# Value products in two matmuls instead of three, a yield in the block sums, and the first head's loads in another order

## The chip, the cores and the metric

The kernel runs on one core of one Trainium2 chip. The metric is device time in microseconds. The kernel before took a median of 2062.04 us over three runs (2061.18 to 2064.16).

## The reference

The program computes a two-layer block over 1024 latent tokens of width 1024, with 256 context tokens ahead of them. The first layer is a bidirectional mLSTM, the second a pooling mixer. The change lies in the first layer, in float32:

```python
def headwise(x, w):                       # w: blocks of 4 x 4
    return jnp.einsum("btgi,gio->btgo", xb, w).reshape(bsz, t, e)

xm, z, og = jnp.split(h @ w_in, 3, axis=-1)
xc = jax.nn.silu(short_conv(xm, conv_w, conv_b))
q = headwise(xc, w_q); k = headwise(xc, w_k) * DH ** -0.5
v = headwise(xm, w_v)
pre = concat([q, k, v]) @ w_g + b_g       # gates: log_i and log_sigmoid
# then, per head, a scan over tokens in both directions with q, k, v and the gates
```

So for each of the 16 blocks of 128 inner channels, 1280 tokens are multiplied by a 128 x 128 block-diagonal matrix (the value) and by 16 columns that give the value's part of the gates.

## The kernel before

**Precision.** A float32 product is made of three matmuls on rounded halves: high by high, high by low, low by high (`mm3`, lines 148 to 151, through `mm`, line 137). `load_w` (lines 139 to 146) loads a weight block and splits it: ACT copies the high half (L143), VectorE (DVE) subtracts it (L145).

**Stage.** The change's first two parts lie in the loop over n = 0 to 15, one n for each block of 128 inner channels. `features(n)` multiplies the weight block with all tokens in three pieces, ci = 0 and 1 of 512 columns and ci = 2 of 256, each 8 steps of k with three matmuls, into PSUM tiles "pa" (three buffers). Each piece is copied by ACT to `xp` (L367) and split into `xmh` (ACT L369) and `xml` (DVE L370). Then follows a convolution along tokens: ACT L372, DVE L373 and L374, ACT L375, and another split (L382, L383). Stores to memory go through the SP queue. Three accumulators `gacc` in "pc" take the gates' columns, six matmuls after each n.

**Tokens.** `token_part(n)` is a generator, stepped from inside `features(n + 1)` (every second k; at n = 2, where two tokens' work is waiting, every k). It goes over ten tiles s of 128 tokens. For each, three matmuls with the token tile as the weights and 144 columns moving (128 of the value matrix, 16 of the gates) fill a third of a PSUM tile "pb" (two buffers). After three s the tile is emptied: ACT copies the high half (L409), DVE subtracts for the low half (L410) and adds the gate columns into `pre` (L411). Both halves are stored (L413).

**Sums.** `block_sums` prepares sums of blocks of h for a later stage: for k = 0 to 3 it loads two tiles (L508), combines them on DVE (L510 to L513), and splits and stores four results (L517 to L519). The loop steps it twice for each n from 2 on. Its tiles, and the token tiles `xmh`, `xml`, come from one pool "S4" of 32 buffers; `xp`, the convolution's result and the value's halves come from "T5", which has five.

**Order.** Each engine runs its instructions strictly in the order of its own queue. That order is not the order of the code: the framework puts each instruction in by its own estimate of when its operands are there, and where a buffer is used again its new user waits for the old one's last reader. So the order of an engine's queue is read from the compiled program.

**First head.** After the stage, `start_head(0)` loads the first 512 tokens of head 0 (L677), `make_A` builds a matrix on DVE, `next_q` makes the queries (L720, L721), the gates' rows are loaded (L691, L698), then the rest of the tokens (`finish_x`, L677 and L671), then values (L685). Scores go into "pa", and DVE multiplies them by the decays (L740) that ACT makes from the gates' rows (L754 to L758).

Of the kernel before, what the change touches and what calls it, by code (L numbers as in the profile page):

```python
# [12 lines left out]
F32R = mybir.dt.float32r  # L13
AF = mybir.ActivationFunctionType
ALU = mybir.AluOpType
AX = mybir.AxisListType

P = 128
# [34 lines left out]
def hybrid_block(ctx: ExitStack, tc: tile.TileContext, xT, ctxT, vecs, w_ada0, w_ada, w_blk, w_krow, blk_mask, w_gate, w_in, b_gate, w_out,  # L53
                 bw_in, bw_pool, bw_out, inv_cnt, outT):
    nc = tc.nc
    V, S, G, PE = nc.vector, nc.scalar, nc.gpsimd, nc.tensor
# [7 lines left out]
    def nm(s):  # L64
        uid[0] += 1
        return f"{s}_{uid[0]}"
# [11 lines left out]
    def tl(tag, shape, dt=F32):  # L78
        n = int(np.prod(shape[1:])) * 4
        assert n <= BYTES[tag], (tag, shape)  # L80
        pool = ph["pool"] if tag in PHASED else sb
        return pool.tile(list(shape), dt, tag=tag, bufs=BUFS[tag], name=nm(tag))
# [3 lines left out]
    def pt_(tag, shape=(P, 512)):  # L86
        return ps.tile(list(shape), F32, tag=tag, bufs=PBUFS[tag], name=nm(tag))
# [4 lines left out]
    def f(t):  # L92
        return t.bitcast(F32)

    def const1(shape, name, dt=F32):
        return ph["pool"].tile(list(shape), dt, name=name)

    def small1(shape, tag, bufs=2, dt=F32):
        return ph["pool"].tile(list(shape), dt, tag=tag, bufs=bufs, name=nm(tag))
# [25 lines left out]
    vh_d = dr.tile([NH, P, 10, DH], F32, name="vh_d")  # L125
    vl_d = dr.tile([NH, P, 10, DH], F32, name="vl_d")
# [9 lines left out]
    def mm(out, lhsT, rhs, start, stop):  # L136
        PE.matmul(out, lhsT, rhs, start=start, stop=stop)  # L137
# [10 lines left out]
    def mm3(out, wh, wl, xh, xl, first, last):  # L148
        mm(out, wh, xh, first, False)
        mm(out, wh, xl, False, False)  # L150
        mm(out, wl, xh, False, last)
# [62 lines left out]
    for kind in LOADS:  # L214
        if kind == "x":
            t = tl("S4", [P, T])
            nc.sync.dma_start(t, xT[:, len(x_sb)])
            x_sb.append(t)
        elif kind == "c":
            t = tl("S4", [P, 4, TC])  # L220
# [13 lines left out]
    for k in range(2):  # L234
# [13 lines left out]
    pre = const1([P, 10, 16], "pre")  # L248
    G.tensor_tensor(pre, bg[:, None, :].to_broadcast([P, 10, 16]), zero1[:, :, None].to_broadcast([P, 10, 16]),
                    op=ALU.add)  # L250
# [138 lines left out]
    def token_part(n, xmh, xml, xch, xcl):  # L389

        bv = small1([P, 32, 4], "bv", 1)
        V.tensor_tensor(bv, mask, wb[:, 2, n:n + 1].to_broadcast([P, 32, 4]), op=ALU.mult)
        bv = bv.rearrange("p a b -> p (a b)")
        vv = small1([P, 2, 144], "vv", dt=F32R)
        V.tensor_copy(vv[:, 0, :P], bv)
        V.tensor_tensor(vv[:, 1, :P], bv, f(vv[:, 0, :P]), op=ALU.subtract)
        V.tensor_copy(vv[:, :, P:], f(gm_all[:, n]).rearrange("p (a b) -> p a b", a=2))
        vh, vl = tl("T5", [P, 10, P], F32R), tl("T5", [P, 10, P], F32R)
        for s0, s1 in ((0, 3), (3, 6), (6, 9), (9, 10)):
            p = pt_("pb", [P, 3, 144])  # L400
            for s in range(s0, s1):
                yield
                if s < 8:
                    ah, al = xmh[0][:, s * P:(s + 1) * P], xml[0][:, s * P:(s + 1) * P]
                else:
                    ah, al = xmh[1][:, (s - 8) * P:(s - 7) * P], xml[1][:, (s - 8) * P:(s - 7) * P]
                mm3(p[:, s - s0], ah, al, vv[:, 0], vv[:, 1], True, True)
            q = p[:, :s1 - s0]
            S.activation(vh[:, s0:s1], q[:, :, :P], AF.Copy)  # L409
            V.tensor_tensor(vl[:, s0:s1], q[:, :, :P], f(vh[:, s0:s1]), op=ALU.subtract)  # L410
            V.tensor_tensor(pre[:, s0:s1], pre[:, s0:s1], q[:, :, P:], op=ALU.add)  # L411
        for t, dst in ((vh, vh_d), (vl, vl_d)):
            nc.sync.dma_start(dst[n // 4, :, :, (n % 4) * P:(n % 4 + 1) * P], f(t))  # L413
        yield

        gx = gx_all[:, n]
        for ci, (o, w) in enumerate(CHUNKS):
            ch, cl = (xch[0][:, o:o + w], xcl[0][:, o:o + w]) if ci < 2 else (xch[1], xcl[1])
            if n == 0:
                mm(gacc[ci][:32, :w], gx, ch, True, False)  # L420
                mm(gacc[ci][:16, :w], gx[:, :16], cl, False, False)
            else:
                mm(gacc[ci][:16, :w], gx[:, :16], cl, False, False)
                mm(gacc[ci][:32, :w], gx, ch, False, n == KE - 1)
# [78 lines left out]
    def block_sums():  # L503

        for k in range(4):
            t0, t1 = tl("S4", [P, T]), tl("S4", [P, T])
            for t, kk in ((t0, k), (t1, k + 4)):
                nc.sync.dma_start(t, h_d[kk])  # L508
            b11, b12, b21, b22 = t0[:, :512], t0[:, 512:], t1[:, :512], t1[:, 512:]
            V.tensor_tensor(b22, b22, b12, op=ALU.subtract)  # L510
            V.tensor_tensor(b12, b12, b11, op=ALU.subtract)
            V.tensor_tensor(b11, b22, b11, op=ALU.add)
            V.tensor_tensor(b21, b21, b11, op=ALU.subtract)  # L513
            yield
            for j, x in ((2, b11), (3, b22), (1, b12), (4, b21)):
                t = tl("S4", [P, 2, 512], F32R)
                S.activation(t[:, 0], x, AF.Copy)  # L517
                V.tensor_tensor(t[:, 1], x, f(t[:, 0]), op=ALU.subtract)
                nc.sync.dma_start(t_d[j - 1, k], f(t))  # L519
                yield  # L520

    side, parts, sums = iter(()), [], block_sums()
    with ctx0:
        for n in range(KE):
            out = features(n, side)
            for _ in side:
                pass
            if n == 2:
                bilinear()
            if n >= 2:  # L530
                for _ in range(2):
                    next(sums, None)
            parts.append(token_part(n, *out))
            if n:
                side = chain(*parts)
                parts = []
# [165 lines left out]
    def make_A(h):  # L702
        ah, al = tl("wh", [P, 4, 32, 4], F32R), tl("wl", [P, 4, 32, 4], F32R)
        r = tl("wr", [P, 4, 32, 4])
        for c in range(4):
            V.tensor_tensor(r[:, c], mask, amat[:, 4 * h + c:4 * h + c + 1].to_broadcast([P, 32, 4]), op=ALU.mult)
        V.tensor_copy(ah, r)
        V.tensor_tensor(al, r, f(ah), op=ALU.subtract)
        return ah.rearrange("p c a b -> p c (a b)"), al.rearrange("p c a b -> p c (a b)")
# [113 lines left out]
    def start_head(h):  # L823
        hd = {}
        fetch_x(hd, h, 0)
        return dict(h=h, hd=hd)

    def next_q(cur, tp):
        return make_q(cur["hd"], cur["A"], tp)

    def finish_x(cur):
        for ci in (1, 2):
            fetch_x(cur["hd"], cur["h"], ci)

    cur = start_head(0)
    cur["A"] = make_A(0)
    cur["q"] = next_q(cur, 0)
    cur["rc"], cur["R"] = load_ctx_gates(0), load_gates(0)
    finish_x(cur)
    fetch_v(cur["hd"], 0, 0, 5)  # L840
    st_prev = st_now = nxt = None
    for i in range(len(seq) + 1):
# [42 lines left out]
        if st and ti == 7:  # L885
            cur = nxt
# [299 lines left out]
    for e, i, n0, n1 in ((V, 0, 0, 4), (G, 1, 2, 4), (V, 1, 0, 2)):  # L1186
        t = yo[i][:, n0:n1]
# [84 lines left out]
```

## Time and profile before

| what | value |
|---|---|
| median of three runs | 2062.04 us |
| the profiled execution's own time | 2061.71 us |
| its span, first to last instruction | 2059.9 us |
| mean granted TensorE clock, share of full | 0.986 |
| TensorE (PE) busy | 1993.8 us, 97% |
| VectorE (DVE) busy | 1244.8 us, 60% |
| ScalarE (ACT) busy | 760.5 us, 37% |
| hardware DMA queue, share of 16 engines | 48.8% |
| chain of waits, share by PE | 87% |

The span is one execution by the hardware profiler, and 1.8 us of the profiled run lie around it. In the timelines a row is one instruction or several equal ones in a row (x2, x3), with its start, its duration and, in brackets, how long its engine was idle before it and what ended that. Matmuls overlap, so that the pace of a stream is read from starts, not from durations.

### The profile page before, as it was taken

How to read it: one execution, taken by the hardware profiler on the slowest of the kernel's cores; microseconds unless marked ns; L12 is line 12 of the kernel's file. 1: busy time of each engine (PE TensorE's matmuls, PEld its weight loads, DVE VectorE, ACT ScalarE, POOL GpSimd, SP SyncE). 2: the span in 40 equal slices, each digit the busy share in tenths (PEclk: the TensorE clock that was granted, in tenths of full speed). 3: DMA queues.
4: the chain of work that ended last, by engine and by line, in shares of the span. 5: the costliest groups of instructions: out<-in, count | busy, mean ns of one | idle time of the engine just before them, and what ended most of it. 6: DMA issues, size and time to landing. Idle time of an engine off the chain costs nothing.

```text
span 2059.9 us, 26957 instructions
## 1 busy us (share of the span) xinstructions
PE 1993.8 (97%) x10210; PEld 1680.1 (82%) x10210; DVE 1244.8 (60%) x2115; ACT 760.5 (37%) x1225; POOL 325.9 (16%) x399
## 2 busy tenths in 40 slices
PE   7899999999999899999999999999999999999997
PEld 5678788888888688888888878887888888888897
DVE  4866566677777577667676662444747293844444
ACT  5444454433333432333323322433423131223443
POOL 4400000042232000000000001343000000001265
PEclk9999999999999999999999999999999999999999
DMA  8476776864444854648355334534331312133573
GB/s 322 159 255 222 261 241 214 303 196 138 148 129 133 269 181 141 227 132 273 98 166 207 108 97 144 197 114 163 103 104 50 102 51 92 46 126 130 181 242 124
DMA packets 201986, 339.48 MB, mean 165 GB/s; under 512 B 12508, under 2 KB 116444, under 8 KB 201856
## 3 DMA queue, kind: packets, MB, share of 16 engines
q1 hardware_dynamic: 201856, 337.76, 48.8%
q8 instruction: 80, 1.31, 0.3%
q14 instruction: 50, 0.41, 0.1%
HBM read 234.77 MB, written 102.94 MB: 164 GB/s over the span
## 4 chain that ended last, share of the span: by engine, by line
PE 87%; DVE 3%; DMA 3%; POOL 1%; ACT 1%; issue 1%; SPq 0%; DVEq 0%; ACTq 0%; POOLq 0%
PE pa L137 45%; PE pc L137 33%; PE pb L137 7%; PE pb L781 1%; DMA wr<-in_w_ada_dram 1%; POOL hn L969 1%; PE pc L812 1%; DVE S L901 1%; DVE wl L145 1%; DMA wr<-in_w_in_dram 1%; DMA T<-in_bw_out_dram 0%; DMA S<-xl_d 0%; POOL S L989 0%; DVE wl L658 0%; DMA S<-h_d 0%
## 5 line engine op out<-in xcount | busy, mean ns | idle before, releaser
L137 PE MATMUL pa<-S,wh 128*128 128x512 f32 (+1 forms) x2496 | 725.9, 375 | 13.8 <-DVE S L312 7.1
L137 PEld LDWEIGHTS pa<-S,wh 128*128 128x128 f32 x2496 | 447.4, 191 | 88.6 <-DVE S L312 10.8
L137 PE MATMUL pa<-S,wl 128*128 128x512 f32 (+1 forms) x1248 | 462.5, 371 | 3.3 <-DVE wl L145 3.3
L137 PE MATMUL pc<-S,wh 128*128 128x512 f32 (+1 forms) x1616 | 451.4, 365 | 4.4 <-ACT wh L143 3.5
L137 PEld LDWEIGHTS pc<-S,wh 128*128 128x128 f32 x1616 | 292.7, 189 | 54.3 <-ACT wh L143 3.7
L145 DVE TENSOR_TENSOR wl<-wr,wh 128x1024 fp32r<-128x1024 f32 (+1 forms) x124 | 147.5, 1189 | 273.0 <-ACT wh L143 272.1
L137 PE MATMUL pc<-S,wl 128*128 128x512 f32 (+1 forms) x808 | 293.8, 365 | 1.0 <-DVE wl L145 1.0
L137 PEld LDWEIGHTS pa<-S,wl 128*128 128x128 f32 x1248 | 237.6, 190 | 44.0 <-DVE wl L145 3.7
L137 PE MATMUL pa<-S,S 128*128 128x512 f32 (+1 forms) x1152 | 250.9, 363 | 10.1 <-DMA S<-xh_d 5.8
L143 ACT ACTIVATE wh<-wr 128x1024 fp32r<-128x1024 f32 (+1 forms) x124 | 124.6, 1005 | 368.6 <-PE pa L137 148.3
L137 PE MATMUL pc<-S,pt 128*128 128x512 f32 x960 | 227.4, 391 | 1.5 <-DVE S L721 1.1
L137 PEld LDWEIGHTS pa<-S,S 128*128 128x128 f32 x1152 | 191.8, 190 | 40.2 <-DMA S<-xh_d 6.2
L137 PEld LDWEIGHTS pc<-S,pt 128*128 128x128 f32 x960 | 178.2, 188 | 38.5 <-DVE S L721 1.7
L137 PEld LDWEIGHTS pc<-S,wl 128*128 128x128 f32 x808 | 152.9, 189 | 25.7 <-DVE wl L145 1.8
L783 ACT ACTIVATE pt<-pb 128x512 fp32r<-128x512 f32 (+1 forms) x96 | 47.7, 523 | 213.8 <-PE pb L781 208.0
L969 POOL TENSOR_TENSOR hn<-hn,pt 128x512 f32<-128x512 f32 (+1 forms) x48 | 77.5, 1617 | 309.0 <-ACT pt L968 307.9
L740 DVE SCALAR_TENSOR_TENSOR T<-pa,T 128x256 f32<-128x256 f32 (+3 forms) x184 | 78.2, 454 | 33.5 <-PE pa L137 29.3
L137 PE MATMUL pb<-S,wh 128*128 128x512 f32 x256 | 78.8, 389 | 0.0
L570 ACT ACTIVATE wh<-T 128x512 fp32r<-128x512 f32 x70 | 41.2, 627 | 96.4 <-PE pc L137 78.3
L794 DVE BATCH_NORM_STATS2 st<-pc 128x6 f32<-128x512 f32 x32 | 22.4, 699 | 86.4 <-PE pc L137 86.4
L145 DVE TENSOR_TENSOR wl<-T,wh 128x1024 fp32r<-128x1024 f32 x32 | 45.5, 1421 | 47.3 <-ACT wh L143 47.2
L137 PEld LDWEIGHTS pb<-vv,S 128*128 128x128 f32 x384 | 61.6, 190 | 11.8 <-ACT S L369 1.9
(319 smaller groups left out, 2371.5 us busy)
## 6 DMA issues: line engine op xcount, KB each, us to landing
wr<-in_bw_in_dram SPq DMA_DIRECT2D x40, 512.0 KB, 3.5
wr<-in_w_in_dram SPq DMA_DIRECT2D x34, 512.0 KB, 4.9
wr<-in_w_ada_dram SPq DMA_DIRECT2D x32, 512.0 KB, 4.0
wr<-in_w_out_dram SPq DMA_DIRECT2D x32, 512.0 KB, 3.5
T<-in_bw_out_dram SPq DMA_DIRECT2D x32, 512.0 KB, 4.3
S<-y_d SPq DMA_DIRECT2D x28, 512.0 KB, 7.0
vh_d<-T SPq DMA_DIRECT2D x16, 640.0 KB, 4.0
vl_d<-T SPq DMA_DIRECT2D x16, 640.0 KB, 6.3
```

The source lines that it names most:

```text
L137: PE.matmul(out, lhsT, rhs, start=start, stop=stop)
L143: S.activation(h, r, AF.Copy)
L145: V.tensor_tensor(l, r, f(h), op=ALU.subtract)
L570: S.activation(hi, a, AF.Copy)
L740: V.scalar_tensor_tensor(W[:, lo + sh:hi + sh], p[:, lo - o:hi - o], 1.0, W[:, lo + sh:hi + sh], op0=ALU.mult, op1=ALU.mult, accum_out=dp[ ...
L781: PE.transpose(p[:, j], st["M"][:, s * P:(s + 1) * P], ident)
L783: S.activation(th[:, :n], p[:, :n], AF.Copy)
L794: V.bn_stats(b6, pv)
L812: PE.transpose(p[:, c], hn[:, c * P:(c + 1) * P], ident)
L901: V.tensor_tensor(b, yraw[kp, hf], f(a), op=ALU.subtract)
L969: G.tensor_tensor(acc, acc, sq, op=ALU.add)
```

## The change

The diff has three parts.

1. In `token_part`, a token tile takes two matmuls: the high half of the tile with both halves of the value matrix side by side, 288 columns, and the low half with the high columns, 144. Each s has its own "pb" tile of 288 columns; ACT copies its first half into a new T5 tile `vst` (L408) and DVE adds the second half to it (L409). When ten are done, DVE adds all gate columns into `pre` at once (L410), ACT copies the high half of the whole token into `vh` (L411), DVE subtracts in place (L412), and both are stored (L414).
2. In `block_sums`, a `yield` stands behind the two loads, and the loop steps the generator three times for each n below 10.
3. `finish_x(cur)` stands ahead of `make_A(0)`, `next_q` and the gates' loads.

From L398 on other lines move by one or two: L508 to L509, L510 to L513 become L512 to L515, L517 to L519 become L519 to L521, L656 becomes L658, L677 becomes L679, L691 and L698 become L693 and L700.

```diff
@@ -395,21 +395,22 @@
         V.tensor_copy(vv[:, 0, :P], bv)
         V.tensor_tensor(vv[:, 1, :P], bv, f(vv[:, 0, :P]), op=ALU.subtract)
         V.tensor_copy(vv[:, :, P:], f(gm_all[:, n]).rearrange("p (a b) -> p a b", a=2))
-        vh, vl = tl("T5", [P, 10, P], F32R), tl("T5", [P, 10, P], F32R)
-        for s0, s1 in ((0, 3), (3, 6), (6, 9), (9, 10)):
-            p = pt_("pb", [P, 3, 144])
-            for s in range(s0, s1):
-                yield
-                if s < 8:
-                    ah, al = xmh[0][:, s * P:(s + 1) * P], xml[0][:, s * P:(s + 1) * P]
-                else:
-                    ah, al = xmh[1][:, (s - 8) * P:(s - 7) * P], xml[1][:, (s - 8) * P:(s - 7) * P]
-                mm3(p[:, s - s0], ah, al, vv[:, 0], vv[:, 1], True, True)
-            q = p[:, :s1 - s0]
-            S.activation(vh[:, s0:s1], q[:, :, :P], AF.Copy)
-            V.tensor_tensor(vl[:, s0:s1], q[:, :, :P], f(vh[:, s0:s1]), op=ALU.subtract)
-            V.tensor_tensor(pre[:, s0:s1], pre[:, s0:s1], q[:, :, P:], op=ALU.add)
-        for t, dst in ((vh, vh_d), (vl, vl_d)):
+        vst, vh = tl("T5", [P, 10, 144], F32R), tl("T5", [P, 10, P], F32R)
+        for s in range(10):
+            yield
+            if s < 8:
+                ah, al = xmh[0][:, s * P:(s + 1) * P], xml[0][:, s * P:(s + 1) * P]
+            else:
+                ah, al = xmh[1][:, (s - 8) * P:(s - 7) * P], xml[1][:, (s - 8) * P:(s - 7) * P]
+            p = pt_("pb", [P, 2, 144])
+            mm(p.rearrange("p a b -> p (a b)"), ah, vv.rearrange("p a b -> p (a b)"), True, False)
+            mm(p[:, 0], al, vv[:, 0], False, True)
+            S.activation(f(vst)[:, s], p[:, 0], AF.Copy)
+            V.tensor_tensor(f(vst)[:, s], f(vst)[:, s], p[:, 1], op=ALU.add)
+        V.tensor_tensor(pre, pre, f(vst)[:, :, P:], op=ALU.add)
+        S.activation(vh, f(vst)[:, :, :P], AF.Copy)
+        V.tensor_tensor(vst[:, :, :P], f(vst)[:, :, :P], f(vh), op=ALU.subtract)
+        for t, dst in ((vh, vh_d), (vst[:, :, :P], vl_d)):
             nc.sync.dma_start(dst[n // 4, :, :, (n % 4) * P:(n % 4 + 1) * P], f(t))
         yield
 
@@ -506,6 +507,7 @@
             t0, t1 = tl("S4", [P, T]), tl("S4", [P, T])
             for t, kk in ((t0, k), (t1, k + 4)):
                 nc.sync.dma_start(t, h_d[kk])
+            yield
             b11, b12, b21, b22 = t0[:, :512], t0[:, 512:], t1[:, :512], t1[:, 512:]
             V.tensor_tensor(b22, b22, b12, op=ALU.subtract)
             V.tensor_tensor(b12, b12, b11, op=ALU.subtract)
@@ -528,7 +530,7 @@
             if n == 2:
                 bilinear()
             if n >= 2:
-                for _ in range(2):
+                for _ in range(3 if n < 10 else 2):
                     next(sums, None)
             parts.append(token_part(n, *out))
             if n:
@@ -833,10 +835,10 @@
             fetch_x(cur["hd"], cur["h"], ci)
 
     cur = start_head(0)
+    finish_x(cur)
     cur["A"] = make_A(0)
     cur["q"] = next_q(cur, 0)
     cur["rc"], cur["R"] = load_ctx_gates(0), load_gates(0)
-    finish_x(cur)
     fetch_v(cur["hd"], 0, 0, 5)
     st_prev = st_now = nxt = None
     for i in range(len(seq) + 1):
```

How the queues stand at three places follows. First, DVE at the end of n = 11: `wl` is the weight block's low half, `pt` the low half of piece ci = 2, T_373 (T_441 in the changed program) the convolution. Before:

```order
L410 TENSOR_TENSOR T_366_2554<-pb_2656,T_365_2553 128x128
L411 TENSOR_TENSOR pre<-pre,pb_2656 128x16
L396 TENSOR_TENSOR vv_2909<-bv_2907,vv_2909 128x128
L392 TENSOR_TENSOR bv_3083<-mask,cst_194 128x128
L145 TENSOR_TENSOR wl_2891<-wr_2887,wh_2889 128x1024
L370 TENSOR_TENSOR pt_2537<-pa_2634,pt_2537 128x256
L373 SCALAR_TENSOR_TENSOR T_373_2686<-T_358_2533,vec,T_373_2686 128x1281
L374 SCALAR_TENSOR_TENSOR T_373_2686<-T_358_2533,vec,T_373_2686 128x1281
L410 TENSOR_TENSOR T_390_2738<-pb_2739,T_389_2737 128x384
L411 TENSOR_TENSOR pre<-pre,pb_2739 128x48
L383 TENSOR_TENSOR S_376_2694<-T_373_2686,S_375_2693 128x1024
L383 TENSOR_TENSOR pt_2692<-T_373_2686,pt_2692 128x256
```

In the changed program, at the same end of n = 11:

```order
L409 TENSOR_TENSOR T_427_2631<-T_427_2631,pb_2746 128x144
L392 TENSOR_TENSOR bv_3174<-mask,cst_194 128x128
L410 TENSOR_TENSOR pre<-pre,T_427_2631 128x160
L145 TENSOR_TENSOR wl_2975<-wr_2971,wh_2973 128x1024
L370 TENSOR_TENSOR pt_2615<-pa_2717,pt_2615 128x256
L412 TENSOR_TENSOR T_427_2631<-T_427_2631,T_428_2632 128x10x128
L373 SCALAR_TENSOR_TENSOR T_441_2771<-T_420_2611,vec,T_441_2771 128x1281
L374 SCALAR_TENSOR_TENSOR T_441_2771<-T_420_2611,vec,T_441_2771 128x1281
L409 TENSOR_TENSOR T_455_2814<-T_455_2814,pb_2822 128x144
L409 TENSOR_TENSOR T_455_2814<-T_455_2814,pb_2833 128x144
L409 TENSOR_TENSOR T_455_2814<-T_455_2814,pb_2844 128x144
L383 TENSOR_TENSOR S_444_2779<-T_441_2771,S_443_2778 128x1024
```

The subtraction of a whole token (L412) now stands between the split of ci = 2 and the convolution, and the adds of the next token's first three tiles (L409) behind the convolution.

Second, DVE at the end of n = 9; S_356 and S_355 are the two loaded tiles of the sums, `pa_2240` and `pa_2291` the pieces ci = 0 and 1 of n = 9. Before:

```order
L392 TENSOR_TENSOR bv_2731<-mask,cst_194 128x128
L145 TENSOR_TENSOR wl_2531<-wr_2527,wh_2529 128x1024
L370 TENSOR_TENSOR pt_2165<-pa_2262,pt_2165 128x256
L373 SCALAR_TENSOR_TENSOR T_324_2314<-T_309_2161,vec,T_324_2314 128x1281
L374 SCALAR_TENSOR_TENSOR T_324_2314<-T_309_2161,vec,T_324_2314 128x1281
L410 TENSOR_TENSOR T_342_2370<-pb_2371,T_341_2369 128x384
L411 TENSOR_TENSOR pre<-pre,pb_2371 128x48
L383 TENSOR_TENSOR S_327_2322<-T_324_2314,S_326_2321 128x1024
L383 TENSOR_TENSOR pt_2320<-T_324_2314,pt_2320 128x256
```

In the changed program:

```order
L410 TENSOR_TENSOR pre<-pre,T_368_2253 128x160
L512 TENSOR_TENSOR S_356_2216<-S_356_2216,S_355_2215 128x512
L145 TENSOR_TENSOR wl_2609<-wr_2605,wh_2607 128x1024
L513 TENSOR_TENSOR S_355_2215<-S_355_2215 128x512
L370 TENSOR_TENSOR pt_2237<-pa_2339,pt_2237 128x256
L412 TENSOR_TENSOR T_368_2253<-T_368_2253,T_369_2254 128x10x128
L514 TENSOR_TENSOR S_355_2215<-S_356_2216,S_355_2215 128x512
L373 SCALAR_TENSOR_TENSOR T_382_2393<-T_361_2233,vec,T_382_2393 128x1281
L515 TENSOR_TENSOR S_356_2216<-S_356_2216,S_355_2215 128x512
L520 TENSOR_TENSOR S_357_2223<-S_355_2215,S_357_2223 128x512
L370 TENSOR_TENSOR S_364_2239<-pa_2240,S_363_2238 128x512
L374 SCALAR_TENSOR_TENSOR T_382_2393<-T_361_2233,vec,T_382_2393 128x1281
```

The sums' four operations (L512 to L515) and a split (L520) now stand among those of this place, the first ahead of the weight block's L145, and the splits of ci = 0 and 1 (L370) come behind them. The changed program has such a place at the ends of n = 5, 7 and 9, and steps sums at the end of n = 3 too; before, they stood at the ends of n = 3, 5, 8 and 10.

Third, the SP queue at the first head; `ab` and `ga_d`, `gb_d` belong to the stage that ends there, `wr` to the conditioning weights. Before:

```order
L610 DMA ga_d<-hn_6014 128x4x128
L691 DMA hn_6087<-a_d 128x256 x2
L654 DMA wr_6489<-in_w_ada_dram 128x1024
L698 DMA S_933_6090<-a_d 128x1024
L610 DMA ga_d<-hn_6038 128x4x128
L698 DMA S_934_6092<-a_d 128x1024
L677 DMA S_935_6094<-xh_d 128x2x512
L677 DMA S_936_6096<-xh_d 128x2x512
L677 DMA S_937_6098<-xl_d 128x2x512
L677 DMA S_938_6100<-xl_d 128x2x512
L671 DMA S_939_6102<-xh_d 128x4x256
```

In the changed program:

```order
L679 DMA S_1021_6170<-xh_d 128x2x512
L679 DMA S_1022_6172<-xh_d 128x2x512
L679 DMA S_1023_6174<-xl_d 128x2x512
L679 DMA S_1024_6176<-xl_d 128x2x512
L612 DMA ga_d<-hn_6043 128x4x128
L673 DMA S_1025_6178<-xh_d 128x4x256
L673 DMA S_1026_6180<-xl_d 128x4x256
L808 DMA ab_6408<-ga_d 128x512
L808 DMA ab_6409<-gb_d 128x512
L808 DMA ab_6554<-ga_d 128x512
L612 DMA ga_d<-hn_6103 128x4x128
L656 DMA wr_6598<-in_w_ada_dram 128x1024
```

The token loads (xh_d, xl_d) have moved ahead of the `ab` loads and the weights; the rows of the gates (a_d, L700) follow after the next weight row, and the context gates (L693) now stand behind four value loads.

## Rows read from the trace of the kernel before

**Rows 1.** Page part 1: busy us (share of span) and instructions of each engine
```profile
PE 1993.8 (97%) x10210; PEld 1680.1 (82%) x10210; DVE 1244.8 (60%) x2115; ACT 760.5 (37%) x1225; POOL 325.9 (16%) x399
```

**Rows 2.** Groups by form, value matmuls: busy, mean ns, idle before
```profile
L137 PE MATMUL pb<-vv,S 128*128 128x144 f32 x384 | 58.6, 261 | 1.6 <-ACT S L369 1.2 <-DVE S L370 0.4
...
L137 PE MATMUL pb<-vv,pt 128*128 128x144 f32 x96 | 14.6, 261 | 0.0
```

**Rows 3.** Timeline, PE, n = 9: start, us, engine, line, operation
```profile
251.35 0.45 PE L137 MATMUL pb<-vv,S 128*128 128x144 f32 x3
...
253.07 0.45 PE L137 MATMUL pb<-vv,S 128*128 128x144 f32 x3
...
258.92 0.40 PE L137 MATMUL pa<-S,wh 128*128 128x256 f32 x2
259.16 0.28 PE L137 MATMUL pa<-S,wl 128*128 128x256 f32 x1
```

**Rows 4.** Timeline of PE, ends of n = 11 and 12
```profile
299.27 1.08 PE L137 MATMUL pc<-S,hn 128*16 128x512 f32 x4
...
300.43 0.63 PE L137 MATMUL pa<-S,wh 128*128 128x512 f32 x2
...
303.18 0.45 PE L137 MATMUL pb<-vv,S 128*128 128x144 f32 x3
...
317.68 1.08 PE L137 MATMUL pc<-S,hn 128*16 128x512 f32 x4
```

**Rows 5.** Timeline, ACT, DVE, SP, end of n = 11
```profile
300.45 1.23 DVE L145 TENSOR_TENSOR wl<-wr,wh 128x1024 fp32r<-128x1024 f32 x1 [0.53 <-ACT wh L143]
...
300.85 1.46 ACT L372 ACTIVATE T<-T,vec 128x1281 f32<-128x1281 f32 x1
...
301.59 0.42 DVE L370 TENSOR_TENSOR pt<-pa,pt 128x256 fp32r<-128x256 f32 x1
301.70 0.55 SPq L141 DMA_DIRECT2D wr<-in_w_in_dram  x1
...
302.34 1.55 DVE L373 SCALAR_TENSOR_TENSOR T<-T,vec,T 128x1281 f32<-128x1281 f32 x1 [0.33 <-ACT T L372]
```

**Rows 6.** Page part 6: DMA issues, KB each, median us to landing
```profile
vh_d<-T SPq DMA_DIRECT2D x16, 640.0 KB, 4.0
vl_d<-T SPq DMA_DIRECT2D x16, 640.0 KB, 6.3
```

**Rows 7.** Timeline of PE, ends of n = 3, 4, 8, 9
```profile
137.41 1.07 PE L137 MATMUL pc<-S,hn 128*16 128x512 f32 x4
...
163.44 1.08 PE L137 MATMUL pc<-S,hn 128*16 128x512 f32 x4
...
237.12 1.08 PE L137 MATMUL pc<-S,hn 128*16 128x512 f32 x4
...
242.82 1.22 PE L137 MATMUL pa<-S,wh 128*128 128x512 f32 x2 [4.38 <-DVE pt L370]
...
262.43 1.08 PE L137 MATMUL pc<-S,hn 128*16 128x512 f32 x4
```

**Rows 8.** Timeline of DVE at the end of n = 8
```profile
238.91 0.69 DVE L510 TENSOR_TENSOR S<-S,S 128x512 f32<-128x512 f32 x1 [1.74 <-DMA S<-h_d]
```

**Rows 9.** Window 242 to 260: busy by engine, PEclk, DMA share
```profile
242.00:260.00 18.00, 17.18 (x82) 14.58 (x83) 11.15 (x18) 8.21 (x14) 0.15 (x3) 0.84 0.62 229
```

**Rows 10.** Timeline of PE, first head
```profile
699.64 1.67 PE L137 MATMUL pa<-S,S 128*128 128x512 f32 x6 [1.95 <-DVE S L721]
...
708.78 0.79 PE L137 MATMUL pa<-S,S 128*128 128x512 f32 x1 [5.82 <-DMA S<-xh_d]
711.49 16.79 PE L137 MATMUL pa<-S,S 128*128 128x512 f32 x76 [1.92 <-DMA S<-xl_d]
```

**Rows 11.** Timeline of ACT, first head
```profile
705.36 0.40 ACT L755 ACTIVATE T<-S,cst 128x128 f32<-128x128 f32 x1 [1.24 <-DMA S<-a_d]
...
707.40 1.15 ACT L757 ACTIVATE T<-S,cst 128x1024 f32<-128x1024 f32 x1 [0.66 <-DMA S<-a_d]
```

## The prediction

> **What bounds the kernel now.** I read the page's first part, then the timelines of TensorE (PE) in the stage of the sixteen n, then those of the other engines where PE stood still. PE is busy 97% of the span [rows 1], so what shortens PE's own stream counts in full, and what delays any other engine counts only where PE runs dry. In the stage the stream is regular: from the gate matmuls that close n = 11 (299.27, called E below) to those that close n = 12 it is 18.41 us [rows 4], without an idle bracket. Two periods are longer: n = 3 to 4 takes 26.03 and n = 8 to 9 takes 25.31 [rows 7], 7.6 and 6.9 us above normal, 14.5 together. At n = 8 PE waited 4.38 for the split of ci = 2 on DVE [rows 7], and DVE had been held 1.74 by the load of an h tile for the sums [rows 8], with L145 and that split queued behind it. After that wait the clock was lower: 0.84 of full over 18 us [rows 9], between the levels of 2.4 and 1.2 GHz, so the rest of the 6.9, 2.5 us, is the clock's.
>
> **Value products.** 480 matmuls of 144 columns [rows 2] in 160 groups of three go; 160 of 288 and 160 of 144 come. From 251.35 to 253.07 six matmuls of 512 and one group pass, 1.72 us [rows 3]; twelve of 512 without a group pass from 300.43 to 303.18, 2.75 us [rows 4], which is 1.375 for six and 0.229 each. A group costs 0.345, a matmul of 144 columns 0.115. One of 256 columns costs 0.12 (258.92 to 259.16 for two) [rows 3]. 288 columns are not shown: they lie between 0.12 and 0.229, and I take 0.134, a straight line between, nearest the 256. So a new group costs 0.249 and saves 0.096: 160 x 0.096 = **-15.4 us** (bounds -17.6 and 0).
>
> The row says that 144 columns cost almost as much as 256, so a matmul has a floor that does not come from its columns. The Trainium skill, "TensorE: Matmul & The Clock Gate", section "Back-to-back issue gap", gives columns / 2.4 + 2.5 ns for a matmul by itself; both groups have 432 columns, so by that alone the change would save 2.5 ns a group, 0.4 us in all. The same section says that the formula falls short at small sizes, where the weight load has a share, and gives 81 ns for 128 columns; the trace's 115 ns for 144 is further in that direction, so I let the trace decide.
>
> **What the new evictions wait for.** Ten ACT copies and ten DVE adds of 144 columns replace eight evictions and four small adds a token; at no more than the 0.42 of the 256-column split [rows 5] that is 4.2 us in 18.4 on either engine, beside PE. Their place matters. At the end of n = 11, counted with the times of before: L145 ends at 301.68, the split of ci = 2 at 302.0 [rows 5]. Then, by the order shown, L412 (1280 columns, put at L373's 1.55) to 303.7, L373 to 305.3, L374, as long, to 306.9, and only then the first L409. PE is ready for tile s = 0 at 303.18 as before [rows 4], for s = 1 at 1.375 + 0.249 later, for s = 2 at 306.4. With two pb buffers s = 2 needs that of s = 0, whose add ends at 306.9 plus some 0.3: a wait of 0.75. There is a second condition. Five T5 buffers serve, and the new `vst` of a token takes the buffer that the previous token's `vh` held, so ACT's L408 of s = 0 waits for that store. The copy L411 now stands at ACT behind the split of n's last piece, so the store is issued at about 302.3, some 0.6 after the weight load at 301.70 [rows 5]. A value store alone lands 4.0 after its issue, one that follows another by 0.6 lands after 6.3 [rows 6]: 306.3 or 308.6. In the second case PE waits 2.7. I take 2.0 of the 0.75 to 2.7, since the store that follows another is the nearer row but a weight load is smaller than a store. Such places are the ends of n = 4, 6, 8, 10 to 14 and, with the last token, 15: nine x 2.0 = **+18.0** (6.8 to 24.3). At n = 2, where a group follows every k, three tiles (s = 2, 4, 7) find an operation of 1.55 ahead of their add; with 0.3 of slack each that is **+3.7** (0 to 9.3).
>
> **The sums.** The `yield` separates load and use by one step of the generator, but both steps are taken in the same n, and with three steps instead of two the sums come at the ends of n = 3, 5, 7, 9. At n = 5, 7 and 9 the changed queue has the form that n = 8 had before: the first sum ahead of L145, the splits of ci = 0 and 1 behind the convolution's L373. Durations: sums and 512-column splits 0.69 [rows 8], L145 1.23, short split 0.42, L373 1.55 [rows 5]. If the load has landed in time, L512 runs from E + 0.6, then L145, L513 and the short split to E + 3.4; PE, ready at E + 1.16 [rows 4], waits 2.3. Its first tile s = 0 comes 2.75 later, at E + 6.2, and needs the split of ci = 0, which stands behind L412, L514, L373, L515 and L520 and ends at E + 9.3: 3.1 more. 5.4 in all, 7.9 with the clock's 2.5. With n = 3 as before: 7.6 + 3 x 7.9 = 31.3, less the 14.5 that go: **+16.8** (+9.3 without the clock; +20 with the load late by 1.7 on top and part of it hidden).
>
> **First head.** PE waits 5.82 for `xh` and 1.92 for `xl` [rows 10]; their loads move ahead of the `ab`, weight and gate loads, and both waits go. What is late next: three "pa" buffers hold three score pieces, 12 x 0.229 twice and 12 x 0.12, done at about 706.5 from 699.64. The fourth needs the first evicted, by a DVE multiply that needs the exponentials of the gates' rows; ACT got these rows at 705.36 and ends the second at 708.55 [rows 11], the multiply (0.69) at about 709.6. These loads keep their place. So PE waits some 3 us there, and at 711.49, where before it had just begun `xl`'s part, it has 11 matmuls of 512 (2.5), 12 of 256 (1.4) and 1.9 us of the next piece behind it: **-6** (-10 if the gates come sooner and the clock stays up; +2 if the context gates, now behind four value loads, hold ACT). The 1.95 for L721 stays.
>
> **Clock.** Of the nine waits of 2.0 I let one be followed by the lower clock, at 2.5: **+2.5** (0 to 22.5).
>
> Sum: -15.4 + 18.0 + 3.7 + 16.8 - 6 + 2.5 = +19.6. On the profiled run's own 2061.7 (span 2059.9 and 1.8 around it) that is 2081.3; on the median of 2062.0, 0.3 higher, 2081.6. I say 2081.5.
>
> **Rivals.** *Even.* The store lands at its lower bound and the lower clock does not follow: 9 x 0.75 = 6.8, sums +9.3, n = 2 at 1.2, products and first head as above: -4.1, 2058. For it: PE stood still nowhere for a T5 buffer before. Against: the order has three long operations ahead of the adds. *Faster.* The yield does what the change says: loads land a step ahead, the splits of ci = 0 and 1 are not held by missing S4 buffers, and the sums' 14.5 go: -15.4 + 3.7 - 14.5 + 12.6 (nine at 1.4) - 6 = -19.6, 2042. For it: the sums at n = 5 and 10 cost nothing before, with the same two loads. Against: there the first sum stood behind L145 and no split of ci = 0 was left. *No saving on PE.* If columns alone set the pace, the products save nothing, and the forecast rises by 15.4 to 2097. The 0.115 against 0.12 speaks against it. *Clock.* Each of the nine waits reaches 2.7 and the granted clock falls after each: -15.4 + 3.7 + 20 + 24.3 + 22.5 - 2 = +53, 2115. The 1.95 wait [rows 10] was below, the 4.38 above the point where that happens.
>
> **Chances and range.** Forecast 0.57, even 0.15, faster 0.16, no saving 0.05, clock 0.07. A measurement of this kernel can tell 0.2%, 4.1 us, from no change. Faster by more than that: the faster rival and half of the even one, 0.23; within it: the rest of the even one and the forecast's low edge, 0.12; slower: 0.65. The forecast's own range is 2066 to 2098; the range over the cases goes from the faster rival's 2042 to 2103, which leaves the clock rival and part of the faster one out.
>
> **What would show it.** Right: a PE start-to-start of 1.62 where a group stands among 512-column matmuls; PE waits on "pb" for DVE L409 of 0.7 to 2.7 us some 7 us after each E; ACT's L408 of s = 0 waiting for the vh_d store; four long periods (n = 3, 5, 7, 9) with PE waiting for L370; no PE wait for `xh_d` near 709, but one for L742. Wrong: periods of 17.5 us at the ends of n = 10 to 14, or L512 running with no split behind it that PE waits for.

## The result, and the profile after

The changed kernel takes a median of 2092.69 us (2090.84 to 2093.25, 4 runs) against 2062.61 us of before (2061.18 to 2064.16, 4 runs). The ratio is 1.0144, 95% interval 1.0127 to 1.0162: about 30 us slower. The forecast was 2081.5 us, 19.6 slower, in a range of 2042 to 2103. Now and then an execution takes far longer than the others of its kernel (below, one of four of e2 and one of four of e11), and such executions are left out of the times.

The page's first part, with the first line of the chain of waits. Answers to [rows 1]:

```profile
PE 1992.4 (95%) x10050; PEld 1668.2 (80%) x10050; DVE 1274.5 (61%) x2179; ACT 790.9 (38%) x1337; POOL 324.5 (16%) x399
...
PE 71%; DVE 3%; DMA 3%; POOL 1%; issue 1%; ACT 1%; SPq 0%; DVEq 0%; ACTq 0%; POOLq 0%
```

PE's busy time fell by 1.4 us while the span grew by 31.6: PE waits more. The share of the chain that PE holds fell from 87% to 71%.

The groups of value matmuls by form (busy, mean ns of one, then the idle time before them). Answers to [rows 2]:

```profile
L137 PE MATMUL pb<-vv,S 128*128 128x288 f32 x128 | 40.5, 316 | 28.2 <-DVE T L409 25.2 <-ACT S L369 2.8
L137 PE MATMUL pb<-vv,S 128*128 128x144 f32 x128 | 30.5, 239 | 4.5 <-DVE S L370 4.5
...
L137 PE MATMUL pb<-vv,pt 128*128 128x288 f32 x32 | 10.5, 327 | 2.1 <-DVE T L409 2.1
L137 PE MATMUL pb<-vv,pt 128*128 128x144 f32 x32 | 7.3, 230 | 0.0
```

480 matmuls have become 320, and the matmuls of 288 columns carry 25.2 and 2.1 us of idle time that ends with DVE's add L409. How large one such wait is stands in PE's timeline, here in the period after the end of n = 4:

```profile
168.88 0.36 PE L137 MATMUL pb<-vv,S 128*128 128x288 f32 x2
...
170.52 0.36 PE L137 MATMUL pb<-vv,S 128*128 128x288 f32 x2
...
174.59 0.47 PE L137 MATMUL pb<-vv,S 128*128 128x288 f32 x2 [2.27 <-DVE T L409]
```

The first two rows are 1.64 us apart, where [rows 3] had 1.72: the saving is there. Then the third tile waits 2.27 us for the add that empties the first tile. Where that comes from, with ACT, DVE and the SP queue beside PE, at the end of n = 11 (E = 321.49; [rows 4, 5] show this place before):

```profile
321.49 1.08 PE L137 MATMUL pc<-S,hn 128*16 128x512 f32 x4
...
323.06 1.28 ACT L411 ACTIVATE T<-T 128x1280 fp32r<-128x1280 f32 x1
...
323.92 0.33 SPq L141 DMA_DIRECT2D wr<-in_w_in_dram  x1
...
324.37 0.53 SPq L414 DMA_DIRECT2D vh_d<-T  x1
324.38 1.49 DVE L412 TENSOR_TENSOR T<-T,T 128x1280 fp32r<-128x1280 f32 x1
...
327.44 1.55 DVE L374 SCALAR_TENSOR_TENSOR T<-T,vec,T 128x1281 f32<-128x1281 f32 x1
...
331.83 0.47 ACT L408 ACTIVATE T<-pb 128x144 f32<-128x144 f32 x2 [6.14 <-DMA vh_d<-T]
332.15 0.52 DVE L409 TENSOR_TENSOR T<-T,pb 128x144 f32<-128x144 f32 x2 [3.16 <-ACT T L408]
...
332.51 0.47 PE L137 MATMUL pb<-vv,S 128*128 128x288 f32 x2 [3.68 <-DVE T L409]
```

ACT's copy L411 ends at 324.34 and the value store is issued at 324.37, behind the weight load of 323.92. DVE has done the subtraction L412 and the convolution by 329.0. Still no add begins: ACT stands 6.14 us idle until 331.83, for the store vh_d of the token before to land, 7.4 us after its issue; behind the weight load it lands after 5.4 to 6.1 us at the other ends of n = 3 to 15. The wait for T5 decides here, then: DVE stands idle 3.16 us behind L374 until ACT has copied. PE loses 3.68 us, the largest of these waits, so that 0.5 of it is left for DVE's order, with L412 and the convolution ahead of the add. The same idle time of DVE behind L374 is 1.76, 1.34, 1.56, 1.51, 3.16, 1.18, 1.44 and 1.89 us at the ends of n = 4, 6, 8 and 10 to 14, 13.8 together, and PE's waits there are 18.0 together: some three quarters are the store's, the rest the order's. The sums of PE's waits in the stage (engine, what it waited for: us, times, longest):

```profile
PE pb L137 <- DVE T L409: 27.4, 25, 3.7
PE pa L137 <- DVE pt L370: 10.9, 4, 4.2
PE pb L137 <- DVE S L370: 4.5, 4, 1.7
PE pb L137 <- ACT S L369: 2.8, 1, 2.8
```

ACT's, in the same window:

```profile
ACT T L408 <- DMA vh_d<-T: 38.9, 9, 6.1
```

Eight of the nine are at the ends named above; the ninth, 1.24 us behind the end of n = 2, held PE nowhere. Before there were 0.4 us of waits on pb for DVE and 1.2 for ACT [rows 2]. PE's period between the gate matmuls of two n, after the ends of n = 4, 6, 8 and 13 (window, length, then busy time by engine; the granted clock is the third number from the end):

```profile
164.97:185.04 20.07, 17.80 (x101) 14.82 (x98) 11.31 (x23) 10.07 (x20) 0.16 (x3) 1.00 0.71 234
210.73:231.94 21.21, 19.35 (x100) 16.02 (x98) 11.39 (x23) 10.18 (x20) 0.16 (x3) 0.92 0.70 223
256.21:276.09 19.88, 17.80 (x100) 14.84 (x98) 11.30 (x23) 10.07 (x20) 0.16 (x3) 1.00 0.72 236
364.95:386.73 21.78, 19.61 (x100) 16.16 (x98) 12.60 (x25) 11.05 (x22) 0.16 (x3) 0.92 0.52 169
```

All four have one wait of about 2 us: 2.27, 1.86, 2.08 and 1.97. Where the granted clock stayed at full, 2.4 GHz, the period is 19.9 to 20.1 us; where it fell for a while to its lower level, 1.2 GHz, it is 21.2 to 21.8. The size of the wait did not decide which.

The places of the sums, ends of n = 5, 7 and 9, PE's first matmul after each:

```profile
189.52 0.72 PE L137 MATMUL pa<-S,wh 128*128 128x512 f32 x2 [3.16 <-DVE pt L370]
...
235.34 0.73 PE L137 MATMUL pa<-S,wh 128*128 128x512 f32 x2 [2.07 <-DVE pt L370]
...
281.58 0.73 PE L137 MATMUL pa<-S,wh 128*128 128x512 f32 x2 [4.17 <-DVE pt L370]
```

These periods take 25.69, 24.27 and 25.10 us, and that of n = 3 takes 26.14; before, only n = 3 and 8 were long [rows 7]. The first sum (L512) was not held at n = 7; at n = 5 DVE stood idle 1.02 us ahead of it, and at n = 9 2.02 us for its load of h_d. So one load was still late here.

The first head, ACT and PE ([rows 10, 11] before):

```profile
735.88 5.14 PE L137 MATMUL pa<-S,S 128*128 128x512 f32 x24
...
744.09 0.60 ACT L722 ACTIVATE S<-pc 128x512 fp32r<-128x512 f32 x1 [7.34 <-PE pc L137]
744.70 1.28 ACT L757 ACT_TABLE_LOAD   x1
...
746.00 0.98 ACT L757 ACTIVATE T<-S,cst 128x128 f32<-128x128 f32 x3
...
746.89 1.14 ACT L759 ACTIVATE T<-S,cst 128x1024 f32<-128x1024 f32 x1
...
748.82 7.42 PE L137 MATMUL pa<-S,S 128*128 128x512 f32 x22 [4.77 <-DVE T L742]
```

The waits for xh_d and xl_d are gone, and one of 4.77 for DVE's multiply by the decays stands in their place. The 1.95 us for L721 is gone too: the stream from 735.88 has no idle time ahead of it. ACT loads the table of its exponential function (ACT_TABLE_LOAD) here as soon as its copy L722 is done, which had waited 7.34 us for PE; the gates' rows were there by then.

### The profile page after: what moved, and what is told of

It is laid out like the page before. It is cut to its first block, busy times and chain, and to the rows that moved or that the text cites. A ratio compares the mean times of both kernels' runs of the same rounds, so it can differ in the third digit from the quotient of the medians.

```text
span 2091.5 us, 26781 instructions
## 1 busy us (share of the span) xinstructions
PE 1992.4 (95%) x10050; PEld 1668.2 (80%) x10050; DVE 1274.5 (61%) x2179; ACT 790.9 (38%) x1337; POOL 324.5 (16%) x399
## 3 DMA queue, kind: packets, MB, share of 16 engines
q8 instruction: 78, 1.28, 0.2%
## 4 chain that ended last, share of the span: by engine, by line
PE 71%; DVE 3%; DMA 3%; POOL 1%; issue 1%; ACT 1%; SPq 0%; DVEq 0%; ACTq 0%; POOLq 0%
PE pa L137 33%; PE pc L137 31%; PE pb L137 5%; PE pb L783 1%; DMA hn<-a_d 1%; PE pc L814 1%; POOL S L991 1%; DMA S<-y_d 0%; DVE S L903 0%; DMA S<-xl_d 0%; DMA wr<-in_w_ada_dram 0%; DMA T<-in_bw_out_dram 0%; POOL S L990 0%; POOL hn L971 0%; DVE S L991 0%
## 5 line engine op out<-in xcount | busy, mean ns | idle before, releaser
L137 PE MATMUL pa<-S,wh 128*128 128x512 f32 (+1 forms) x2496 | 729.5, 377 | 19.9 <-DVE pt L370 10.9
L145 DVE TENSOR_TENSOR wl<-wr,wh 128x1024 fp32r<-128x1024 f32 (+1 forms) x124 | 146.5, 1182 | 271.0 <-ACT wh L143 270.1
L785 ACT ACTIVATE pt<-pb 128x512 fp32r<-128x512 f32 (+1 forms) x96 | 47.9, 523 | 217.9 <-PE pb L783 212.1
L409 DVE TENSOR_TENSOR T<-T,pb 128x144 f32<-128x144 f32 x160 | 45.6, 300 | 70.5 <-ACT T L408 70.2
L408 ACT ACTIVATE T<-pb 128x144 f32<-128x144 f32 x160 | 44.1, 292 | 113.0 <-PE pb L137 73.8
L137 PEld LDWEIGHTS pb<-vv,S 128*128 128x128 f32 x256 | 47.0, 194 | 49.6 <-DVE T L409 32.3
L137 PE MATMUL pb<-vv,S 128*128 128x288 f32 (+1 forms) x256 | 50.6, 277 | 32.7 <-DVE T L409 25.2
```

The source lines that it names most:

```text
L145: V.tensor_tensor(l, r, f(h), op=ALU.subtract)
L408: S.activation(f(vst)[:, s], p[:, 0], AF.Copy)
L409: V.tensor_tensor(f(vst)[:, s], f(vst)[:, s], p[:, 1], op=ALU.add)
L785: S.activation(th[:, :n], p[:, :n], AF.Copy)
```

## The experiments

Each kernel is the one before with the edit shown; times are compared with runs of the kernel before on the same chip.

**The parts alone.** e1 has the token part of the diff, e2 the yield and the third step, e3 the moved `finish_x`.

```diff
# e1: lines 398 to 413 as in the diff
# e2
+            yield                      # behind the two loads of h_d
-                for _ in range(2):
+                for _ in range(3 if n < 10 else 2):
# e3
     cur = start_head(0)
+    finish_x(cur)
     cur["A"] = make_A(0)
...
-    finish_x(cur)
```

Expected of e1: 

> Only the value products and their evictions are changed (part 1); sums and first head as before. Theory A (the tile vst takes the buffer of the previous token's vh, so the first ACT copy waits for a store that is now issued behind a weight load): the saving of about 10 us on TensorE is outweighed by waits of about 2 us on pb at some ten places and by a lower clock after some of them; 15 to 23 us slower than before, with nine or so ACT waits for DMA vh_d. Rival B (the loss of the changed kernel is that of the sums, and the products only save): 8 to 15 us faster.

Expected of e2: 

> Only the yield in the block sums and the third step (part 2). Theory A (the sums then stand at the ends of n = 3, 5, 7, 9 in the form that n = 8 had before, with the first sum ahead of the weight block's L145 and the splits of ci = 0 and 1 behind): four long periods of about 25 us instead of two, 11 to 16 us slower. Rival B (the load comes a step ahead, the DMA wait on DVE goes): the two long periods go, 7 to 14 us faster.

Expected of e3: 

> Only the first head's loads in the other order (part 3). Theory A: PE's waits for xh_d and xl_d (7.7 us) go, one of 3 to 5 us for DVE's multiply by the decays comes, 4 to 8 us faster. Rival B (the end of the stage is set by the gates' rows, which keep their place): within 2 us of before.

Measured: e1 1.0117 (1.0099 to 1.0134), some 24 us slower; e2 1.0044 (1.0027 to 1.0061), 9 slower; e3 0.9977 (0.9967 to 0.9986), 5 faster. Their sum, 28.5, is close to the 30 of the whole. So the value products, which were to save time on PE, are the larger part of the loss. Waits of PE in e1's stage, and of ACT in the next fence:

```profile
PE pb L137 <- DVE T L409: 27.4, 27, 2.3
```

```profile
ACT T L408 <- DMA vh_d<-T: 42.6, 11, 4.8
```

That is theory A, with the same 27.4 us of pb waits as in the changed kernel; rival B is out, and the loss was a little above the upper end that A gave.

In e2 the long periods are four, as theory A has it, though two of them are 22.8 us and not about 25, and the loss of 9 us is below its 11 to 16. The end of n = 5 (E = 183.79), DVE and PE:

```profile
183.75 0.68 DVE L511 TENSOR_TENSOR S<-S,S 128x512 f32<-128x512 f32 x1
...
185.44 1.22 DVE L145 TENSOR_TENSOR wl<-wr,wh 128x1024 fp32r<-128x1024 f32 x1
...
187.18 0.42 DVE L370 TENSOR_TENSOR pt<-pa,pt 128x256 fp32r<-128x256 f32 x1
...
187.65 1.22 PE L137 MATMUL pa<-S,wh 128*128 128x512 f32 x2 [2.54 <-DVE pt L370]
...
190.18 1.28 DVE L370 TENSOR_TENSOR S<-pa,S 128x512 fp32r<-128x512 f32 x2
```

L511 starts before E, with no idle time ahead of it: the load is in time, so rival B's cause is removed, and yet PE stands still 2.54 us. What holds it is the row of operations ahead of the short split (187.18). At n = 7 the load was late by 0.7 and the clock lower for longer:

```profile
183.79:206.58 22.79, 20.25 (x110) 17.01 (x108) 16.16 (x32) 12.58 (x21) 0.16 (x3) 0.93 0.71 254
225.02:249.69 24.67, 21.37 (x110) 17.85 (x108) 16.21 (x32) 12.45 (x21) 0.16 (x3) 0.86 0.65 235
```

The period after the end of n = 9 is 22.79 as well. Rival B is out: where the load was on time the period was long all the same.

In e3 theory A held, with a new wait a little above its 3 to 5 us. What ends last now is the gates' rows, and then something the prediction had not counted, ACT's table load:

```profile
706.88 1.28 ACT L755 ACT_TABLE_LOAD   x1 [0.74 <-DMA S<-a_d]
...
710.98 13.91 PE L137 MATMUL pa<-S,S 128*128 128x512 f32 x55 [5.48 <-DVE T L740]
```

Before, ACT had made that table load early, behind the context gates that it had waited for:

```profile
701.52 1.28 ACT L756 ACT_TABLE_LOAD   x1 [4.12 <-DMA hn<-a_d]
```

**The wait for the store taken away.** e4 is e1 with a buffer for vst that no store reads.

```diff
-    BUFS = {"S4": 32, ...
+    BUFS = {"S4": 31, ...
-        vst, vh = tl("T5", [P, 10, 144], F32R), tl("T5", [P, 10, P], F32R)
+        vst = ph["pool"].tile([P, 10, 144], F32, tag="vs", bufs=1, name=nm("vs"))
+        vh, vl = tl("T5", [P, 10, P], F32R), tl("T5", [P, 10, P], F32R)
...
-        V.tensor_tensor(vst[:, :, :P], f(vst)[:, :, :P], f(vh), op=ALU.subtract)
-        for t, dst in ((vh, vh_d), (vst[:, :, :P], vl_d)):
+        V.tensor_tensor(vl, vst[:, :, :P], f(vh), op=ALU.subtract)
+        for t, dst in ((vh, vh_d), (vl, vl_d)):
```

Expected: 

> Part 1 alone, but vst has a buffer of its own that is stored from nowhere: the low half is written to a second T5 tile, and both halves are stored from T5. S4 has 31 buffers instead of 32 to make room. Theory A (the wait for the store makes the loss of part 1): no ACT wait for vh_d, the pb waits shrink below 0.8 us, and the kernel is 5 to 12 us faster than before, some 25 us faster than part 1 alone. Rival B (the order on DVE, L412 and the convolution ahead of the adds, makes it): the waits stay at 1 to 2 us and it is 0 to 10 us slower than before.

Measured: 1.0036 (1.0024 to 1.0047), 7.6 us slower than before and 17 faster than e1. ACT waits for no store any more, and PE's waits for the add:

```profile
PE pb L137 <- DVE vs L410: 9.8, 17, 1.6
```

From 27.4 to 9.8 us. But e4 changed a second thing: in its queue two of the adds (here L410) stand ahead of the convolution's L374, where the changed kernel has them behind it. At the end of n = 11 (E = 321.03), DVE:

```profile
326.78 0.30 DVE L410 TENSOR_TENSOR vs<-vs,pb 128x144 f32<-128x144 f32 x1
...
327.51 1.55 DVE L374 SCALAR_TENSOR_TENSOR T<-T,vec,T 128x1281 f32<-128x1281 f32 x1
```

So the 17 us are of both together; the store's part is read from DVE's idle time in the changed kernel, three quarters of the waits at the eight ends. As forecasts, neither theory held whole: A's cause was the larger one, but A had the kernel faster than before and the waits below 0.8 us, and the time and the longest wait of 1.6 lie where rival B put them. Two of e4's periods say why it did not become faster than before:

```profile
221.67:239.15 17.48, 17.48 (x101) 14.93 (x98) 11.32 (x24) 10.35 (x20) 0.16 (x3) 1.00 0.78 250
239.15:266.44 27.29, 20.90 (x100) 16.69 (x98) 17.91 (x34) 13.93 (x27) 0.16 (x3) 0.87 0.59 207
```

The first, after the end of n = 7, is the only one without any wait: 17.48 us, 0.94 less than the 18.42 of before, 0.094 a group. The others, but for those of n = 3 and 8, are 17.9 to 18.8: a single idle time of 0.2 us on pb near the end of a period goes with some 0.45 of its length, one of 0.9 with 1.3. The second, after the end of n = 8, is longer than before's 25.3, and that of n = 3 (27.35) longer than 26.0: PE's waits on pb for the splits, of up to 3.1 us, join the sums there. The last token's period grew too, from 12.77 to 15.54.

**The sums in another place.** e5 is e2 with one more step of the generator at n = 1, so that loads and sums fall in different n.

```diff
-            if n >= 2:
-                for _ in range(3 if n < 10 else 2):
+            if n:
+                for _ in range(1 if n == 1 else 3 if n < 10 else 2):
```

Expected: 

> Part 2 with one extra step at n = 1, so that the loads of a k stand at one n and its four sums at the next; all else as before. Theory A (what costs is where the framework puts the sums on DVE and that splits wait for S4 buffers; here the sums stand behind the weight block's L145 and no split of ci = 0 or 1 is left behind): the long period of n = 8 goes, the one of n = 3 goes or shrinks, 5 to 14 us faster. Rival B (four sums on DVE at a boundary cost some 4 us wherever they stand): 2 us faster to 8 us slower.

Measured: 0.9923 (0.9908 to 0.9938), 16 us faster than before. The periods after the ends of n = 3 and n = 8:

```profile
137.82:156.22 18.40, 18.40 (x110) 15.82 (x108) 11.76 (x24) 10.33 (x17) 0.15 (x3) 1.00 0.87 287
229.90:248.34 18.44, 18.44 (x111) 15.84 (x108) 14.08 (x28) 10.22 (x17) 0.15 (x3) 1.00 0.80 288
```

PE is busy from end to end in both, where before they had taken 26.0 and 25.3. Theory A, with a gain a little above its 14 us. DVE after the end of n = 8 (E = 229.90):

```profile
232.22 0.42 DVE L370 TENSOR_TENSOR pt<-pa,pt 128x256 fp32r<-128x256 f32 x1
...
233.11 0.69 DVE L511 TENSOR_TENSOR S<-S,S 128x512 f32<-128x512 f32 x1 [0.47 <-DMA S<-h_d]
```

The first sum stands behind the short split here, and even waits 0.47 us for its load, and the period is not longer. Rival B is out: four sums at a boundary cost nothing if the weight block's split and the other splits are not behind them.

**One S4 buffer less, and the parts joined.** e6 is the kernel before with 31 S4 buffers (`"S4": 31`), the control for e4; e7 is e4 with e3's edit; e8 is e4, e5's two edits and e3's.

Expected of e6: 

> The kernel before with 31 S4 buffers instead of 32. Theory A (one buffer less costs little; the rest of e4's loss lies in its own waits): 0 to 3 us slower than before. Rival B (the missing buffer is what keeps e4 above before): 5 to 10 us slower, with long periods of 27 us at the ends of n = 3 and 8.

Expected of e7: 

> e4 (own buffer for vst) and the first head's loads in the new order. Theory A (the parts add up): 3.6 us less than e4, about 4 us slower than before. Rival B (e4's gates' stage ends later, so that the loads are early anyway): no gain on e4.

Expected of e8: 

> e4's own buffer, e5's sums a step ahead, and the first head's new order together. Theory A (parts add up, and the long periods of n = 3 and 8, 9 us each in e4, go): 10 to 20 us faster than before. Rival B (with two waits gone the next one, for splits or the single vst buffer, ends last): within 5 us of before.

Measured: e6 1.0007 (0.9997 to 1.0016), no change that can be told; e7 1.0029 (1.0018 to 1.0040), 1.5 less than e4, so less than the 3.6 that theory A gave and inconclusive between the two; e8 0.9956 (0.9940 to 0.9973), 9 us faster than before, between what its two theories gave, and 7 slower than e5, which has only the sums. How much of that the products cost is not shown by e8 alone, since it has one S4 buffer less as well (see e11).

**The best so far, and the products only where they run alone.** e9 is e5 with e3's edit. e10 is e8 with the three matmuls and the shared tile of before for n = 0, 1 and 15 (`if 2 <= n <= 14:` around the new form). e11 is e9 with 31 S4 buffers.

Expected of e9: 

> e5's sums a step ahead and the first head's new order, value products as before. Theory A (they meet at no common wait): e5 and e3 add up, 18 to 20 us faster than before, about 2043. Rival B (the head's gain needs the end of the stage to be late): like e5, 2046 to 2047.

Expected of e10: 

> e8, but the tokens n = 0, 1 and 15 keep the three matmuls and the shared tile of before; only n = 2 to 14 have the two matmuls. Theory A (e8 loses at n = 2, where two tokens run together, at the last token and behind it, and saves 0.5 us in each n between): 3 to 7 us faster than e9, about 2037 to 2040. Rival B (the products' later end costs the stage behind it whatever the first and last tokens do): 2046 to 2054.

Expected of e11: 

> e9 with 31 S4 buffers, as e10 needs them. Theory A (the first head's loads wait for S4 buffers, and the missing one costs e10 its saving): 2 to 4 us slower than e9, 2044 to 2046. Rival B (the buffer costs nothing, as in e6; e10 loses elsewhere): 2041 to 2043.

Measured: e9 2042.09 us, ratio 0.9905 (0.9891 to 0.9919), 20 us faster than before and the best of all: theory A. e10 2044.59, 0.9914 (0.9898 to 0.9929): no better than e9, between its two theories. e11 2050.11, 0.9946 (0.9927 to 0.9966): 8 us slower than e9 from the one buffer, more than theory A gave. So in e10 the two matmuls save some 6 us against e11, and the buffer that pays for vst costs more than that. e8 and e11, with 31 buffers both, cannot be told apart, so that over all sixteen n no saving and no cost of the products in two matmuls is shown. PE's wait at the first head, e9:

```profile
696.19 14.64 PE L137 MATMUL pa<-S,S 128*128 128x512 f32 x57 [5.11 <-DVE T L741]
```

and e11:

```profile
699.25 20.33 PE L137 MATMUL pa<-S,S 128*128 128x512 f32 x93 [6.93 <-DVE T L741]
```

1.8 of the 8 us are in this one wait. The profiled executions differ by 5.1 us in their spans (2040.9 and 2046.0), and four more of PE's waits are longer in e11: for ACT's L772 (2.8 against 1.9), for DVE's L785 (1.3 more), for the loads of in_w_ada (12.4 against 11.6) and for DVE's L491 (0.6 against none). In e6 the waits for ACT's copy (L771 there) and for L491 are as long as in e11, but its wait for the split at n = 8 is 3.4 where before had 4.4. Why one buffer less moves these places is not shown.

## Why the prediction was right, step by step

- **Direction and mechanism.** Slower, by waits on pb for the add L409, by the store behind the weight load, and by four places of the sums. e1 and e2 show the products and the sums each by itself. The store is shown by ACT's nine waits for it and by DVE's idle time behind L374; e4, which took the wait away, moved the adds too. The argument that a late load is what the sums cost (the "faster" rival) falls with e2, where the load was in time and the period long.
- **Value products, -15.4.** A period without a wait is 17.48 against 18.42 (e4): 0.094 a group, 15.0 us over 160 groups. By the column formula of the Trainium skill ("TensorE: Matmul & The Clock Gate", section "Back-to-back issue gap"), which is for a matmul by itself, a group would save an estimated 0.0025 us; the trace's 0.094 decides against it.
- **Nine waits, +18.0.** The largest pb waits after the ends of n = 4, 6, 8 and 10 to 14 are 2.27, 1.86, 2.08, 2.03, 3.68, 1.71, 1.97 and 2.41, and the last token has 1.57 and 0.93: 20.5 in all. The 2.0 each was near, 2.25 on average at the first eight, though one (n = 11) was above the bound of 2.7: there the store took 7.4 us, above the 6.3 that the bound came from. Why it took longer there than at n = 10, with the same neighbours in the queue, is not shown. Both conditions that the prediction named were at work at these eight, with 13.8 us for the store and the rest for DVE's order. The last token's waits are not the store's: ACT waits for no store there, and they are the same in e4 (1.57 and 0.95).
- **Third token tile at n = 2, +3.7.** Waits of 1.46, 0.94 and 0.91, 3.3 together, and the same in e4.
- **Sums, +16.8.** Periods 26.14, 25.69, 24.27 and 25.10, each less 17.48, are 31.3, less the 14.5 of before: 16.8. That it comes out to the figure is luck: PE's first wait was to be 2.3 and is 2.07 at n = 7, but 3.16 and 4.17 at n = 5 and 9, where the first sum was held; the second, for the split of ci = 0, was to be 3.1 and is 0.53, 1.72 and 0.53. This sum is of places. Part 2 alone costs 9; in the changed kernel L412 stands in the row at these places too (189.38 to 190.86 at n = 5), but what each thing adds was not separated.
- **First head, -6.** e3 measures -4.7 (-6.8 to -2.9). The term was too large: the wait that took the place of the old ones is 4.8 to 5.5 us, not 3. ACT's table load of 1.28 us is a part of that: before, it ran behind the context gates (701.52), ahead of the gates' rows (705.36); now it stands ahead of the first exponential, behind the gates' rows in e3 and behind the copy L722 in the changed kernel. Against it, the 1.95 for L721, which the prediction let stay, is gone in both.
- **Clock, +2.5: mis-sized.** The prediction let one wait in nine be followed by the lower clock. Three were, n = 6, 11 and 13. Their periods, less 17.48 and the wait, are longer by 1.87, 2.34 and 2.33: 6.5. By the granted clock of 0.92, 0.93 and 0.92 in these periods, an estimated 5.1 of it is the clock's. And the periods without it, less 17.48 and the wait, are 0.3 to 0.8 longer each, with the last token's 1.2 some 4.2 us; brackets show at most 0.3 of each, and no term held this. The rival on the clock had a point between waits of 1.95 and 4.38 us from which the clock falls; it fell after 1.86 and not after 2.41, so the length of the wait alone does not decide.
- **The sum.** -15.0 + 20.5 + 3.3 + 16.8 - 4.7 + 6.5 + 4.2 = 31.6; the spans of the profiled executions differ by 31.6, the medians by 30. The 6.5 and the 4.2 are remainders of periods, so the agreement is no proof of them. The 12 us between the forecast's 19.6 and this sum are small delays that no term held (4.2, and the 1.4 of the 6.5 that is not the clock's), the clock (2.6), the nine waits (2.5) and the first head (1.3).

What stays open: why one buffer less costs e11 8 us where e6 could spare it, and what sets after which of two waits alike the clock falls.

## What to carry to other kernels

When a tile's copy or store moves from every few steps to the end of a unit of work, ask which buffer the next unit's first write takes, and when that buffer's last reader, a store too, will have landed; the saving is on the busy engine, the wait beside it. A generator's `yield` moves work only to where the loop steps it, and where an engine's operations land is read from its queue, not from the code. An experiment that takes one wait away can move the queue as well, so its order is read again before the gain is put down to the wait. A change of three parts is to be measured in parts: here two lost, one gained, and the idea behind one of the losing parts, carried through (e5), was worth 16 us.

## What the runs showed of the hardware that was not expected

- The granted clock fell after waits of 1.86, 1.97 and 3.68 us (0.92 to 0.93 over the period) and not after waits of 2.03, 2.08, 2.27 and 2.41 (1.00).
- A value store of 640 KB, which landed 4.0 us after its issue in the kernel before, where the weight load came behind it [rows 6], took 5.4 to 6.1 between a weight load and a second store, and 7.4 once.
- A matmul of 288 columns costs little more than one of 144: 0.094 us (periods of 17.48 and 18.42) of the 0.115 that the third matmul of a group had cost is saved.
